# The PSUM banks that the transposes of v use in a gated DeltaNet and attention step

## The chip, the cores and the metric

One core of a Trainium2 chip runs the whole kernel. The metric is the device time of one execution in microseconds (us); the kernel before is given by the median of three executions.

## The reference

One inference step of a two-layer decoder trunk, for a prompt of 512 tokens and a sample group of 8 x 4 tokens that share the weights. Layer 0 is a gated DeltaNet, layer 1 a sliding-window attention, and each is followed by a SwiGLU block. The change lies in layer 0, which computes, cut to what matters:

```python
proj = h @ w_in                                   # 1024 -> q, k, v (8, 8, 16 heads of 128), z, b, a
qkv = silu(sum(full[:, k:k + L] * w[k] for k in range(4)))   # short causal convolution
q, k = l2norm(q) * 128 ** -0.5, l2norm(k)
Bm = strict(kb @ k.T * decay)                     # kb = k * beta, per chunk and head
T = inverse(I + Bm)                               # by doubling: M = -Bm, T = I + M, T += T @ M^(2^i)
u, w = T @ (v * beta), T @ (kb * exp(G))
for each chunk:                                   # the state S goes from chunk to chunk
    unew = u - w @ S
    o = (q * exp(G)) @ S + aqk @ unew
    S = S * exp(Gl) + (k * exp(Gl - G)).T @ unew
out = (rmsnorm(o) * silu(z)) @ w_out
```

## The kernel before, in words

Tokens lie along the free axis (544 columns: 512 of the prompt, 32 of the samples), cut into two halves of 256 and 288. Every large product is `dense` (L142): weights come in pieces of 128x512 over the SyncE queue, ScalarE rounds them to a high part and VectorE makes the low part (L133), and TensorE adds three products per weight block into one PSUM bank per half (L161). Tiles share the buffers in SBUF and the eight PSUM banks by tags. In the DeltaNet layer (L258) the banks are: `acc` three, for the halves of the projections; `t` two; `c` two; `v` one.

The DeltaNet work is cut into four groups g of two q/k heads and four v heads. Each group goes through steps, and the text `PLAN` (L39, L40) says in which order the steps are written down for all groups:

- kq (L587): the projections of k and q, each followed by `conv_silu` (L543): copies out of PSUM into a buffer `pre` (two of them), four taps into a buffer `y` (three of them; L559 on ScalarE, L561 on VectorE), a tanh (L563), and SiLU products (L571).
- t (L606): transposes of k and q, the Gram blocks with their decay (L692 to L705), the inverses of the 16x16 diagonal blocks on GpSimd, and for the samples a doubling product of 128x128 (L756 to L770). All of its PSUM tiles have the tag `t`; the last three are `pm`, `pm2` and `pm3`. `M1` (L765) is the sum that VectorE reads out of `pm2`, `TTs` (L770) the sum out of `pm3`. The small tiles MT, Mn and M1 have the SBUF tag `s128` with three buffers, which the sample step uses too (`rs`, L987).
- p and s (L920, L970): the products of the samples with their states, fed as small pieces between the blocks of other projections, and the rest of the samples' step.
- m (L774): the merge of the diagonal blocks into the inverse of 128x128. It is a chain of small products with a copy after each; its ten PSUM tiles all have the tag `v`, so each waits for the copy of the one before. Its last copy is L836.
- v (L838): for each of four heads a projection and `conv_silu`, whose result stays in `y`; four transposes of 128x128 into one bank `pv` (L849 to L851); and four copies by ScalarE, scaled by beta, into Vb (L854). Only then is `y` free. Vb is read by the chain of chunks.
- c (L857): the chain of the four chunks, with the tag `c`; z and o (L1024, L1041): the gate's projections and the output, of which z uses `pre` and no `y`.

The order on each engine is not that of the plan alone. The program writes the steps down in plan order, and a scheduler, which is told to use its own estimate of all durations (L1562), puts the instructions of each engine in an order in which steps overlap. Each engine then works strictly in that order, with waits on semaphores. A tile waits until a buffer of its tag is free. The lines around the change:

```python
PLAN = ("ba kq0 rn gt t0 p0 kq1 v0 s0 m0 t1 p1 c0 v1 kq2 z0 o0 s1 m1 t2 "
        "p2 c1 v2 kq3 z1 o1 s2 m2 t3 c2 v3 p3 z2 z3 o2 s3 m3 c3 wa wb o3")
```

Of the kernel before, what the change touches and what calls it, by code (L numbers as in the profile page):

```python
# [399 lines left out]
def gdn(ctx, tc, env):  # L400
    nc, PE, DVE, ACT, POOL = (env[k] for k in ("nc", "PE", "DVE", "ACT", "POOL"))
    tmp, bank, dense, halves = (env[k] for k in ("tmp", "bank", "dense", "halves"))
# [140 lines left out]
    def conv_silu(m, slot, cso, scst, emit, r=None):  # L543
        ps = dense(w_in[m], f"win{m}", hrhs, [8])
        pre = tmp("pre", f"pre{m}")
        pres = pre[:, YS:CONVW].rearrange("p (b t) -> p b t", t=3 + NT)
        POOL.memset(pre[:, 0:3], 0.0)
        POOL.tensor_copy(pres[:, :, 0:3], scst[:, slot].rearrange("p (b t) -> p b t", t=3))
        ACT.copy(pre[:, 3:3 + CUT], ps[0][:, :CUT])
        ACT.copy(pre[:, 3 + CUT:3 + SEQ], ps[1][:, :SEQ - CUT])  # L550
        ACT.copy(pres[:, :, 3:], ps[1][:, SEQ - CUT:TOK - CUT].rearrange("p (b t) -> p b t", t=NT))
        if r is not None:
            DVE.tensor_tensor(pre[:, 3:3 + SEQ], pre[:, 3:3 + SEQ], r[:, :SEQ], ALU.mult)
            DVE.tensor_tensor(pres[:, :, 3:], pres[:, :, 3:],
                              r[:, SEQ:].rearrange("p (b t) -> p b t", t=NT), ALU.mult)
        POOL.tensor_copy(cso[:, slot, 0:3], pre[:, SEQ:SEQ + 3])
        POOL.tensor_copy(cso[:, slot, 3:].rearrange("p (b t) -> p b t", t=3), pres[:, :, 4:7])
        y = tmp("y", f"y{m}")
        ACT.activation(y[:, :YW], pre[:, 0:YW], AF.Identity, scale=pc("taps", m * 4))  # L559
        for k in range(1, 4):  # L560
            DVE.scalar_tensor_tensor(y[:, :YW], pre[:, k:k + YW], pc("taps", m * 4 + k), y[:, :YW], ALU.mult, ALU.add)  # L561
        th = pre
        ACT.activation(th[:, :YW], y[:, :YW], AF.Tanh, scale=0.5)  # L563

        def srows(t):
            return t[:, YS:CONVW].rearrange("p (b t) -> p b t", t=3 + NT)[:, :, :NT]

        return emit(th, y, srows(th), srows(y))

    def sil(out, th, y):  # L570
        DVE.scalar_tensor_tensor(out, th, 1.0, y, ALU.add, ALU.mult)  # L571
# [266 lines left out]
    def proj_v(q):  # L838
        g = q.g
        q.Vb = [p2.tile([P, 4, P], F32, tag="Vb", name=f"Vb{g}_{n}", bufs=VBB) for n in range(NCH)]  # L840
        q.VS = p2.tile([P, 4, NB, NT], F32, tag="VS", name=f"VS{g}")
        for h in range(4):
            def emit(th, y, ths, ys):
                sil(q.VS[:, h], ths, ys)
                sil(y[:, :SEQ], th[:, :SEQ], y[:, :SEQ])
                return y

            VT = conv_silu(16 + 4 * g + h, 4 + h, q.cso, q.scst, emit)
            pv = bank("v", f"pv{g}_{h}")  # L849
            for n in range(NCH):  # L850
                PE.transpose(pv[:, n * P:(n + 1) * P], VT[:, n * P:(n + 1) * P], ident)  # L851
            for n in range(NCH):
                cc = n * 16 + 4 * g + h
                ACT.mul(q.Vb[n][:, h, :], pv[:, n * P:(n + 1) * P], col["bh"][:, cc:cc + 1])  # L854
        nc.gpsimd.dma_start(cs_out[:, 8 * g:8 * g + 8], q.cso)
# [272 lines left out]


    steps = {"kq": proj_kq, "t": tphase, "v": proj_v, "p": states, "s": sample, "m": merge, "c": chain, "z": proj_z, "o": out}  # L1130
    groups = {}
    for step in PLAN.split():
# [10 lines left out]
        else:  # L1143
            g = int(step[-1])
# [422 lines left out]
```

## Time and profile before

| what | value |
| --- | --- |
| median of three executions | 1694.58 us (1690.14 to 1696.34) |
| the profiled execution | 1703.09 us, of which its span is 1701.3 us |
| TensorE busy | 1634.9 us, 96% of the span |
| VectorE, ScalarE, GpSimd busy | 942.4, 753.6, 178.9 us |
| mean granted TensorE clock | 0.972 of full speed |

The span runs from the first to the last instruction of the profiled execution, and all places in the text are us from its start. In the tables PE is TensorE (PEld its weight loads, which overlap its products), DVE is VectorE, ACT is ScalarE, POOL is GpSimd. A row of a timeline has the start in us, the time that the merged instructions took, engine, line, operation, written tile and read tiles, shape and count; in brackets stands how long the engine was idle before and for whom it waited. The DeltaNet layer takes roughly the first 650 us.

### The profile page before, as it was taken

The numbers are of one execution on the slowest core, as the hardware profiler recorded it, in microseconds if no ns is written. First come the engines' busy times: TensorE is split into PE (matmuls) and PEld (weight loads), VectorE is DVE, ScalarE is ACT, GpSimd is POOL, SyncE is SP. The second block draws the span as 40 slices with busy tenths as digits, with TensorE's granted clock in tenths as the row PEclk, the third lists the DMA queues.
The fourth block names the chain that finished last, engine by engine and source line by source line (L and its number), as shares of the span: only waits on it lengthen the run. The fifth ranks groups of instructions, "written<-read, shape, count | busy, mean of one in ns | idle before, by whom it ended". The sixth has DMA issues, their size and how long they took to land.

```text
span 1701.3 us, 36800 instructions
## 1 busy us (share of the span) xinstructions
PE 1634.9 (96%) x14778; PEld 1574.8 (93%) x14778; DVE 942.4 (55%) x2089; ACT 753.6 (44%) x1826; POOL 178.9 (11%) x387
## 2 busy tenths in 40 slices
PE   7998988999999999999999999999999999999997
PEld 6898687898898898999999999999789999999997
DVE  6994574775656546554545433457666454544333
ACT  5765466665675354433333322246554333333221
POOL 3433132132121100100000000100000000000001
PEclk9999699999999999999999999999899999999998
DMA  6234333534436556523232333453112232223332
GB/s 230 77 109 120 107 73 124 155 62 161 145 81 186 175 148 194 183 87 93 88 88 88 87 87 91 125 146 117 28 50 82 88 87 87 88 90 90 87 90 82
DMA packets 156828, 186.06 MB, mean 109 GB/s; under 512 B 60928, under 2 KB 85552, under 8 KB 156656
## 3 DMA queue, kind: packets, MB, share of 16 engines
q1 hardware_dynamic: 148112, 161.98, 33.3%
q0 software_dynamic: 4416, 15.19, 2.5%
q10 hardware_dynamic: 4128, 6.53, 1.3%
q8 instruction: 116, 1.90, 0.5%
q14 instruction: 56, 0.46, 0.1%
HBM read 153.92 MB, written 24.49 MB: 105 GB/s over the span
## 4 chain that ended last, share of the span: by engine, by line
PE 82%; DMA 5%; DVE 4%; issue 3%; ACT 2%; POOL 2%; SPq 1%; POOLq 0%; ACTq 0%; DVEq 0%
PE wg_p L161 16%; PE wu_p L161 16%; PE wd_p L161 14%; PE win_p L161 6%; PE wo_p L161 6%; PE wz_p L161 4%; PE wqkv_p L161 4%; PE wao_p L161 3%; PE ptp L1296 1%; PE po L1302 1%; PE gram L692 1%; PE wdl_p L374 1%; DMA wk<-ksd 1%; PE pu L895 1%; PE po L866 1%
## 5 line engine op out<-in xcount | busy, mean ns | idle before, releaser
L161 PE MATMUL wu_p<-hl,wh_wu 128*128 128x256 f32 (+1 forms) x704 | 199.7, 288 | 0.0
L161 PE MATMUL wg_p<-hl,wh_wg 128*128 128x256 f32 (+1 forms) x704 | 199.7, 288 | 0.0
L161 PE MATMUL wg_p<-hh,wl_wg 128*128 128x256 f32 (+1 forms) x704 | 199.2, 287 | 0.0
L161 PE MATMUL wu_p<-hh,wl_wu 128*128 128x256 f32 (+1 forms) x704 | 199.1, 287 | 0.0
L161 PE MATMUL wg_p<-hh,wh_wg 128*128 128x256 f32 (+1 forms) x704 | 198.5, 288 | 0.3 <-DVE g L331 0.3
L161 PE MATMUL wu_p<-hh,wh_wu 128*128 128x256 f32 (+1 forms) x704 | 198.8, 288 | 0.0
L161 PE MATMUL wd_p<-al,wh_wd 128*128 128x256 f32 (+1 forms) x660 | 190.4, 289 | 0.0
L161 PE MATMUL wd_p<-ah,wl_wd 128*128 128x256 f32 (+1 forms) x660 | 190.1, 288 | 0.0
L161 PE MATMUL wd_p<-ah,wh_wd 128*128 128x256 f32 (+1 forms) x660 | 188.1, 285 | 0.0
L137 DVE TENSOR_TENSOR wl_wd<-wr_wd,wh_wd 128x512 fp32r<-128x512 f32 x90 | 58.3, 647 | 151.7 <-ACT wh_wd L135 150.6
L161 PE MATMUL win_p<-hl0n,wh_win 128*128 128x256 f32 (+1 forms) x448 | 136.9, 307 | 1.6 <-DVE hl0n L280 1.4
L161 PE MATMUL win_p<-hh0n,wl_win 128*128 128x256 f32 (+1 forms) x448 | 133.9, 302 | 2.5 <-DVE wl_win L137 2.5
L161 PE MATMUL win_p<-hh0n,wh_win 128*128 128x256 f32 (+1 forms) x448 | 135.2, 304 | 0.0
L135 ACT CAST wh_wg<-wr_wg 128x512 fp32r<-128x512 f32 x88 | 54.6, 620 | 178.9 <-PE wu_p L161 130.8
L161 PEld LDWEIGHTS wg_p<-hh,wh_wg 128*128 128x128 f32 x704 | 132.3, 188 | 0.4 <-DVE g L331 0.4
L161 PEld LDWEIGHTS wg_p<-hh,wl_wg 128*128 128x128 f32 x704 | 132.6, 189 | 0.0
L161 PEld LDWEIGHTS wu_p<-hh,wl_wu 128*128 128x128 f32 x704 | 132.6, 189 | 0.0
L161 PEld LDWEIGHTS wu_p<-hh,wh_wu 128*128 128x128 f32 x704 | 132.4, 188 | 0.0
L161 PEld LDWEIGHTS wg_p<-hl,wh_wg 128*128 128x128 f32 x704 | 132.4, 188 | 0.0
L161 PEld LDWEIGHTS wu_p<-hl,wh_wu 128*128 128x128 f32 x704 | 132.4, 188 | 0.0
L135 ACT CAST wh_wd<-wr_wd 128x512 fp32r<-128x512 f32 x90 | 52.7, 585 | 174.8 <-PE wd_p L161 153.7
L161 PEld LDWEIGHTS wd_p<-al,wh_wd 128*128 128x128 f32 x660 | 124.1, 188 | 0.0
(467 smaller groups left out, 4462.0 us busy)
## 6 DMA issues: line engine op xcount, KB each, us to landing
wr_wg<-in_w_gu SPq DMA_DIRECT2D x88, 256.0 KB
wr_wu<-in_w_gu SPq DMA_DIRECT2D x88, 256.0 KB
wr_wd<-in_w_dn SPq DMA_DIRECT2D x75, 256.0 KB
wr_win<-in_w_in SPq DMA_DIRECT2D x64, 256.0 KB
Sgp<-in_sdelta SPq DMA_DIRECT2D x16, 512.0 KB
Sgs<-in_sdelta SPq DMA_DIRECT2D x16, 512.0 KB
wr_wz<-in_w_in SPq DMA_DIRECT2D x32, 256.0 KB
out_ss<-Sgs POOLq DMA_DIRECT2D x16, 512.0 KB, 4.5
```

Of the source, the lines that this page charges most:

```text
L135: ACT.copy(hi[:, :n], raw[:, o:o + n])
L137: DVE.tensor_tensor(lo[:, :n], raw[:, o:o + n], hi[:, :n], ALU.subtract)
L161: PE.matmul(ps[f][:m, :hw(f)], lhsT=wt[:, sl], rhs=xt[:, hc(f)], start=(k0 + j == 0 and wi == 0), stop=(k0 + j == total - 1 and wi == 2),)
L374: PE.matmul(p, lhsT=wt[i][:, sl], rhs=xt[k][:, c], start=(k == 0 and wi == 0), stop=(k == KF - 1 and wi == 2))
L692: PE.matmul(gr[:, j * 256:(j + 1) * 256], lhsT=KQ[j][:, n, 0, :], rhs=KQ[j][:, n].rearrange("p a b -> p (a b)"), start=True, stop=True)
L866: PE.matmul(po[:, h * P:(h + 1) * P], lhsT=q.BA[n // 2][:, n % 2, h, 1, :], rhs=un[:, h], start=True, stop=True)
L895: PE.matmul(pu[:, h * P:(h + 1) * P], lhsT=q.BA[n // 2][:, n % 2, h, 0, :], rhs=V[:, h], start=True, stop=True)
L1296: PE.transpose(ptp[:, c * 256 + kb * P:c * 256 + (kb + 1) * P], s[:, c, n, kb * P:(kb + 1) * P], ident)
L1302: PE.matmul(po[rows, n * P:(n + 1) * P], lhsT=vt[:, n - 1 + kb, kv * 64:kv * 64 + 64], rhs=pT[:, c, kb * P:(kb + 1) * P], start=(kb == k0 ...
```

## The change

The four transposes of a v head go into a bank with the tag `t`, of which there are two, in place of the one with the tag `v`. Everything else stays: the pools, the plan, the merge, which is then alone on `v` after the start.

```diff
             VT = conv_silu(16 + 4 * g + h, 4 + h, q.cso, q.scst, emit)
-            pv = bank("v", f"pv{g}_{h}")
+            pv = bank("t", f"pv{g}_{h}")
             for n in range(NCH):
                 PE.transpose(pv[:, n * P:(n + 1) * P], VT[:, n * P:(n + 1) * P], ident)
```

## Rows read from the trace of the kernel before

**Rows 1.** The page: span, and busy time of the engines (share of the span, count).

```profile
span 1701.3 us, 36800 instructions
...
PE 1634.9 (96%) x14778; PEld 1574.8 (93%) x14778; DVE 942.4 (55%) x2089; ACT 753.6 (44%) x1826; POOL 178.9 (11%) x387
```

**Rows 2.** Busy time by stretches; first the length, PEclk is the mean granted clock.

```profile
core 0: us, PE busy (x) PEld busy (x) DVE busy (x) ACT busy (x) POOL busy (x), PEclk, DMA share, GB/s
98.00:123.00 25.00, 25.00 (x241) 23.26 (x240) 23.11 (x38) 16.19 (x42) 6.90 (x15) 1.00 0.45 131
157.00:171.00 14.00, 7.77 (x212) 6.70 (x210) 4.14 (x23) 5.29 (x10) 0.31 (x1) 0.86 0.60 133
171.00:212.00 41.00, 38.03 (x475) 28.09 (x475) 22.94 (x60) 18.63 (x49) 7.41 (x15) 0.63 0.36 110
212.00:235.00 23.00, 19.08 (x145) 18.21 (x145) 16.73 (x40) 17.06 (x60) 12.97 (x43) 1.00 0.23 29
300.00:361.00 61.00, 61.00 (x532) 55.82 (x531) 47.19 (x108) 41.86 (x120) 10.44 (x31) 1.00 0.43 126
361.00:368.00 7.00, 7.00 (x57) 6.89 (x56) 4.87 (x15) 5.77 (x19) 5.98 (x17) 1.00 0.12 38
```

**Rows 3.** Timeline of TensorE: the first transposes of v of groups 0 to 3.

```profile
98.30 0.60 PE L851 MATMUL pv<-kon,y 128*128 128x128 f32 x4
...
207.38 0.60 PE L851 MATMUL pv<-kon,y 128*128 128x128 f32 x4
...
333.45 0.49 PE L851 MATMUL pv<-kon,y 128*128 128x128 f32 x3
...
469.11 0.60 PE L851 MATMUL pv<-kon,y 128*128 128x128 f32 x4
```

**Rows 4.** Timeline of ScalarE: v0's last Vb copies, v1's first tanh, m0's last copy.

```profile
123.33 1.14 ACT L854 ACTIVATE Vb<-pv,c_bh 128x128 f32<-128x128 f32 x4 [1.12 <-PE pv L851]
...
125.48 0.68 ACT L563 ACTIVATE pre<-y 128x568 f32<-128x568 f32 x1
...
206.45 0.56 ACT L836 COPY BA<-py 64x512 f32<-64x512 f32 x1
```

**Rows 5.** Timelines of TensorE, VectorE and ScalarE: users of the tag s128.

```profile
131.83 0.38 PE L985 MATMUL pk<-kon,ksT 128*128 128x128 f32 x2
...
146.02 0.29 DVE L770 TENSOR_TENSOR TTs<-pm,MT 128x128 f32<-128x128 f32 x1 [2.47 <-PE pm L767]
...
146.19 0.36 ACT L987 ACTIVATE rs<-pk,c_bh 128x128 f32<-128x128 f32 x1
```

**Rows 6.** Timeline of ScalarE: copies of half projections, and the taps of v1's fourth head.

```profile
134.28 0.37 ACT L549 COPY pre<-win_p 128x256 f32<-128x256 f32 x1
...
209.03 0.79 ACT L559 ACTIVATE y<-pre,par 128x568 f32<-128x568 f32 x1
...
361.23 0.37 ACT L549 COPY pre<-win_p 128x256 f32<-128x256 f32 x1 [0.79 <-PE win_p L161]
```

**Rows 7.** Timeline of TensorE: the last projection product before the gap, the first after it.

```profile
163.56 0.36 PE L161 MATMUL win_p<-hh0n,wl_win 128*128 128x256 f32 x1
...
218.27 0.38 PE L161 MATMUL win_p<-hh0n,wh_win 128*128 128x288 f32 x1
```

**Rows 8.** Timeline of VectorE: the sum M1 of t0 to t3.

```profile
142.92 0.29 DVE L765 TENSOR_TENSOR M<-pm,MT 128x128 f32<-128x128 f32 x1
...
213.58 0.28 DVE L765 TENSOR_TENSOR M<-pm,MT 128x128 f32<-128x128 f32 x1
...
364.13 0.28 DVE L765 TENSOR_TENSOR M<-pm,MT 128x128 f32<-128x128 f32 x1
...
498.30 0.29 DVE L765 TENSOR_TENSOR M<-pm,MT 128x128 f32<-128x128 f32 x1
```

**Rows 9.** VectorE in a convolution: line L561 (ns min/median/max, starts), then two SiLU products.

```profile
L561 DVE SCALAR_TENSOR_TENSOR y<-pre,par,y x96: 791/802/812, 34.9 to 473.5; 128x568 f32<-128x568 f32 x96
...
126.19 0.19 DVE L571 SCALAR_TENSOR_TENSOR VS<-pre,y 128x32 f32<-128x32 f32 x1 [0.28 <-ACT pre L563]
126.31 0.68 DVE L571 SCALAR_TENSOR_TENSOR y<-pre,y 128x512 f32<-128x512 f32 x1
```

## The prediction

> **What bounds the kernel now.** I read the page first: TensorE is busy for 1634.9 of 1701.3 us [rows 1], so the end moves when TensorE's idle time, or its time at half clock, moves. The busy time by stretches shows where that is [rows 2]: 157 to 171 us has 14.00 - 7.77 = 6.2 us idle, 171 to 212 has 3.0 us idle and a mean granted clock of 0.63 (1.2 GHz for most of it, 2.4 GHz for the rest), 212 to 235 has 3.9 us idle. From 300 to 368 it is never idle.
>
> Why 157 to 235? Follow the transposes of v on TensorE [rows 3] and the rows ahead of them on ScalarE [rows 4]. Group 0's first transposes run at 98.30, as soon as their input is there. For group 1 the tanh of the first head ends at 125.48 + 0.68 = 126.2 and the only v bank is free at 123.33 + 1.14 = 124.5, yet the transposes wait until 207.38, behind the merge's last copy out of that bank (206.45 + 0.56 = 207.0). So a bank goes to the tiles of its tag in program order, whoever is ready first: m0 stands ahead of v1. The SBUF tag s128 says the same: `rs` of s0 has its input at 131.83 + 0.38 and runs at 146.19, right after t0's last tile user ends at 146.02 + 0.29 [rows 5]. While v1's transposes wait, three y buffers are held; the fourth head's taps run at 209.03 [rows 6], and no projection matmul runs between 163.56 and 218.27 [rows 7].
>
> **The change, part by part.** Nothing is added or removed: 64 transposes and 64 scaled copies as before. Their banks change, and with order of allocation the thing waited for: v(g) stands behind all of t(g) in the plan, so its first transposes need the bank that t(g)'s second doubling product frees, when its sum M1 has been read: 143.2, 213.9, 364.4 and 498.6 [rows 8], in place of 98.30, 207.38, 333.45 and 469.11 [rows 3]. All four are later: by 44.9, 6.5, 31.0 and 29.5 us. The merge gains nothing: when m(g) asks for its bank, v(g)'s last copies are long done, as for m0 (124.5).
>
> Price of a freed y: one convolution is taps 0.79 [rows 6], three multiply-adds of 0.80 [rows 9], tanh 0.68 [rows 4], two SiLU products of 0.68 and 0.19 [rows 9]: 4.7 us at least, before its `pre` buffer and then accumulator banks come free.
>
> *Group 0.* Three heads hold the y's; v0's fourth and v1's first sit in `pre`; v1's second fills two accumulators and half of v1's third the last, which came out at 134.28 [rows 6]. From there dense stands until 143.2 + 0.6 + 4.7 = 148.5: a hole of 14.2 us. I cost it at nothing, because the same four projections (they too end where the buffers are full) then run in 164 to 207, where dense has none now. Without that cover it is 14.2. Ends: 0 and +14; below zero is the second rival.
>
> *Group 1.* Release moves from 207.38 to 213.9, +6.5. Against it, t0 has VectorE more to itself (23.11 of 25.00 us busy at 98 to 123 [rows 2], with convolutions that now wait). For it, t1 must start after v0's last transposes: 148.5 + 0.6 in place of 146.3, +2.8. Ends: -6 (as far as t1 could run ahead) and +9. I take +3, nearer to the row of M1 than to the unseen speed-up.
>
> *Group 2.* Dense is at 100% here [rows 2], so a hole costs. The last half projection that fits came out at 361.23 [rows 6]; the y comes at 364.4 + 0.6, the `pre` at 369.7: a hole of 8.5 us. About half is filled by c1, which stands between t2 and v2 in the plan, is under way then, and would otherwise take TensorE later. I take +4; ends 0 (t2 ahead by as much) and +12 (no cover, and the clock falls: after the idle of 157 to 171 it stood at 0.63 over 41 us).
>
> *Group 3.* Behind v3 come z2 and z3, which need no y and can go on with the other `pre` buffer; Vb of group 3 is read by c3, after m3. Taken as 0, ends -1 and +3.
>
> *Two banks.* What could be gained directly is that a head's transposes no longer wait for the copies of the head before. In group 0 heads come one projection apart, so nothing waits. In group 1 three waits of at most 1.14 us [rows 4] could go. The Trainium skill (Perfetto Trace Analysis, section Matmuls) advises that independent groups rotate through PSUM banks so that one's evacuation overlaps the next one's matmuls. By that rule the sum would be 3.4 us less, +4 in place of +7; the trace agrees with the rule only where a bank is what is waited for, and that is an earlier tile of another step, not the neighbour. I take 0.
>
> Sum: 0 + 3 + 4 + 0 = **+7 us**. Made against the profiled execution, that is 1703.1 to 1710; against the median of the runs, 1694.6 (8.5 less), it is **1702**. With the ends of the terms its own range is about 1695 to 1709: some ends exclude each other, since a faster t0 helps both group 0 and group 1.
>
> **The rivals.** A measurement of this kernel can tell about 0.5%, 8.5 us: under 1686 is faster, over 1703 slower.
>
> *The hole of group 0 is not made up.* Place: 134 to 149. If the projections that move to 150 and later get between m0's steps and push m0 and t1 by as much, the 14.2 us stay: 1702 + 14 = 1716. For it: TensorE is full from 98 to 123 [rows 2] and works in its order, so each piece put in front of a merge step delays it. Against: 9.2 us idle and the half clock in 157 to 212 leave room. 0.20.
>
> *Faster: t0 and m0 move up.* Convolutions of three heads (v0's last, v1's first two) leave VectorE before 143, 3 x (2.4 + 0.68 + 0.19) = 9.8 us. If all of it shortens t0, then m0, which hangs on t0 through the DMAs of its blocks, and t1, which is woven into m0, end 9.8 us sooner: release at 213.9 - 9.8 = 204.1, 3.3 us ahead of now, and the projections fill the gaps at 157 to 171, so that the clock may hold. At 0.63 over 41 us up to 0.37 x 41 = 15 us are at stake; taking half, 3 + 7 = 10 us: 1685. It decides from the point where t1's M1 comes over 6.5 us earlier than 213.9. For it: VectorE at 92% in 98 to 123. Against: nothing shows that t0 waits for VectorE alone. 0.17.
>
> *The change does not do what I say: banks go to whoever is ready.* Then v1 is transposed at about 127, the y's come free and projections fill 164 to 218: idle 6.2 + 3.0 + 3.9 = 13 us and some half clock, so about 1680. Against it are the waits of rows 4 and 5. 0.03.
>
> *Nothing shows.* All the holes fall into waits that are there anyway, or t2 runs ahead as far as its cover went: 1694.6, give or take 3. For it: half of my sum is under the spread of the runs. 0.15.
>
> **How the numbers follow.** My forecast has 0.45: of its range 1695 to 1709 a little over half lies within 0.5% (0.26), the rest above (0.19). The first rival adds 0.20 to slower; the faster one 0.14 to faster and 0.03 to same; the third 0.03 to faster; the fourth 0.15 to same. Faster 0.17, same 0.44, slower 0.39. The range, 1688 to 1718, runs from the upper part of the faster rival to a little over the first; about 2 in 10 is left out.
>
> **What would show it.** In the changed profile, v's first transposes come just after the M1 sum of their own group's t step, at about 143, 210 to 214, 360 to 364 and 498; the taps of v0's fourth head move past 140; TensorE shows a hole near 134 to 149 and a smaller one near 361 to 370; 157 to 212 holds more projection matmuls. I am wrong if v1's transposes run before 200, if TensorE stays full at 134 to 149, or if m0's last copy (206.45) comes over 6.5 us sooner or later.

## The result and the profile after

The changed kernel takes 1724.23 us (median of four executions, 1719.41 to 1725.54), the kernel before 1695.46 us (four, 1690.14 to 1698.39): their medians lie 28.8 us, 1.7%, apart. The ratio on record for the pair is 1.0133, 95% interval 1.0094 to 1.0171, and the text goes by it: slower by about 1.3%, some 23 us by that ratio and 29 at the upper end of its interval, where I had forecast 7 us. The profiled execution took 1725.54 us, its span 1723.7.

The page after, answering to [rows 1]:

```profile
span 1723.7 us, 36805 instructions
...
PE 1635.9 (95%) x14778; PEld 1575.1 (91%) x14778; DVE 944.9 (55%) x2089; ACT 754.7 (44%) x1826; POOL 187.4 (11%) x387
```

TensorE works as long as before (1635.9 against 1634.9 us) in a span 22.4 us longer, so nearly all of the loss is idle time of TensorE. The busy time by stretches, columns as in [rows 2], shows where it lies. First after, then three stretches of the kernel before that [rows 2] doesn't have:

```profile
123.00:157.00 34.00, 22.62 (x153) 19.54 (x152) 18.62 (x39) 19.46 (x64) 14.57 (x40) 0.80 0.23 52
157.00:171.00 14.00, 10.10 (x189) 9.03 (x187) 4.90 (x11) 7.69 (x32) 1.48 (x6) 1.00 0.59 140
171.00:212.00 41.00, 36.36 (x575) 30.86 (x576) 21.15 (x69) 18.21 (x41) 7.70 (x17) 0.83 0.43 141
212.00:235.00 23.00, 19.23 (x132) 15.70 (x133) 16.07 (x40) 19.26 (x68) 7.36 (x20) 1.00 0.10 13
300.00:361.00 61.00, 61.00 (x602) 55.71 (x602) 41.25 (x108) 41.21 (x113) 9.91 (x24) 1.00 0.40 124
361.00:381.00 20.00, 13.89 (x120) 12.18 (x119) 13.65 (x33) 13.44 (x48) 11.05 (x33) 0.91 0.20 37
381.00:425.00 44.00, 38.62 (x381) 36.78 (x380) 28.50 (x56) 22.80 (x60) 10.25 (x15) 0.89 0.51 138
```

```profile
123.00:157.00 34.00, 34.00 (x283) 33.16 (x282) 21.26 (x45) 23.85 (x83) 13.06 (x45) 1.00 0.41 104
361.00:381.00 20.00, 19.99 (x158) 19.58 (x157) 13.22 (x33) 11.11 (x32) 11.39 (x35) 1.00 0.27 51
381.00:425.00 44.00, 41.33 (x718) 39.08 (x717) 24.88 (x52) 24.39 (x87) 9.79 (x18) 0.92 0.52 162
```

Two new holes: 34.00 - 22.62 = 11.4 us idle at 123 to 157, where TensorE had been full, and 6.1 us at 361 to 381, with 2.7 us more than before at 381 to 425. From 157 to 235 the idle time is 12.3 us, against 13.1 before: as idle time the first hole is hardly given back, though from 171 to 212 the mean granted clock is higher, 0.83 against 0.63.

The holes lie where the order of allocation puts them. TensorE's first transposes of v in groups 0 to 3, answering to [rows 3]:

```profile
137.43 1.92 PE L851 MATMUL pv<-kon,y 128*128 128x128 f32 x8
...
227.42 1.21 PE L851 MATMUL pv<-kon,y 128*128 128x128 f32 x8
...
369.52 0.60 PE L851 MATMUL pv<-kon,y 128*128 128x128 f32 x4
...
517.27 0.60 PE L851 MATMUL pv<-kon,y 128*128 128x128 f32 x4
```

and VectorE's sums M1 of t0 to t3, answering to [rows 8]:

```profile
136.50 0.29 DVE L765 TENSOR_TENSOR M<-pm,MT 128x128 f32<-128x128 f32 x1 [1.63 <-PE pm L763]
...
226.00 0.28 DVE L765 TENSOR_TENSOR M<-pm,MT 128x128 f32<-128x128 f32 x1
...
367.93 0.28 DVE L765 TENSOR_TENSOR M<-pm,MT 128x128 f32<-128x128 f32 x1
...
513.11 0.29 DVE L765 TENSOR_TENSOR M<-pm,MT 128x128 f32<-128x128 f32 x1 [0.95 <-PE pm L763]
```

In every group the transposes run 0.9 to 4.2 us after the M1 of their own group, and 20 to 48 us later than before. Group 0's first input (the SiLU product of its first head) ends at 95.50, as before (95.33), and its transposes come 39 us later. In the kernel before they did not quite run as soon as the input was there, but 3 us after it. What follows on ScalarE in group 0, answering to [rows 6] and to m0's last copy of [rows 4]:

```profile
112.33 0.37 ACT L549 COPY pre<-win_p 128x256 f32<-128x256 f32 x1 [0.66 <-ACT E L704]
...
139.54 0.78 ACT L559 ACTIVATE y<-pre,par 128x568 f32<-128x568 f32 x1
140.20 1.16 ACT L854 ACTIVATE Vb<-pv,c_bh 128x128 f32<-128x128 f32 x4
141.21 0.81 ACT L559 ACTIVATE y<-pre,par 128x568 f32<-128x568 f32 x1
...
146.13 0.37 ACT L549 COPY pre<-win_p 128x256 f32<-128x256 f32 x1
...
213.10 0.58 ACT L836 COPY BA<-py 64x512 f32<-64x512 f32 x1 [1.54 <-PE py L835]
```

No half projection is copied out between 112.7 and 146.13. The last projection products before each hole and the first behind it, on TensorE:

```profile
128.94 0.28 PE L161 MATMUL win_p<-hh0n,wl_win 128*128 128x256 f32 x1
...
147.78 0.59 PE L161 MATMUL win_p<-hh0n,wh_win 128*128 128x288 f32 x1
...
363.25 0.28 PE L161 MATMUL win_p<-hh0n,wl_win 128*128 128x256 f32 x1
...
381.64 0.61 PE L161 MATMUL win_p<-hh0n,wh_win 128*128 128x288 f32 x1
```

The projections stand still for 18.6 us in group 0 and 18.1 us in group 2, where I had worked out 14.2 and 8.5.

### The profile page after: what moved, and what is told of

Read it like the earlier page. It is cut to its first block, busy times and chain, and to the rows that moved or that the text cites. A ratio compares the mean times of both kernels' runs of the same rounds, so it can differ in the third digit from the quotient of the medians.

```text
span 1723.7 us, 36805 instructions
## 1 busy us (share of the span) xinstructions
PE 1635.9 (95%) x14778; PEld 1575.1 (91%) x14778; DVE 944.9 (55%) x2089; ACT 754.7 (44%) x1826; POOL 187.4 (11%) x387
## 4 chain that ended last, share of the span: by engine, by line
PE 80%; DMA 6%; DVE 5%; POOL 3%; ACT 2%; issue 2%; SPq 1%; POOLq 0%; ACTq 0%; DVEq 0%
PE wg_p L161 15%; PE wu_p L161 15%; PE wd_p L161 14%; PE win_p L161 8%; PE wo_p L161 6%; PE wqkv_p L161 4%; PE wz_p L161 4%; PE wao_p L161 3%; POOL LT L741 1%; POOL subt L739 1%; PE po L1302 1%; DMA Sgp<-in_sdelta 1%; PE wdl_p L374 1%; PE ptp L1296 1%; PE gram L692 1%
```

## The experiments

Runs of the kernel before scatter by some 25 us among themselves (1684 to 1709 us over one series of 35). So verdicts rest on the timed ratios with their 95% intervals, and the traces, one execution each, tell places and orders; the traced execution of the kernel before is one of its longer ones (1703.09 us).

**One group at a time.** The change for one group alone; `g == 0` becomes 1, 2 and 3 in the others.

```diff
-            pv = bank("v", f"pv{g}_{h}")
+            pv = bank("t" if g == 0 else "v", f"pv{g}_{h}")
```

> Only group 0's transposes of v use the banks of the t step, groups 1 to 3 keep the merge's bank. Theory 1 (transposes now stand behind the whole t step of their group; the projections stop where the three y buffers are held, and that costs only where nothing else makes it up): the hole at about 129 to 146 us is there as in the changed kernel, but it is made up before 235, so the time is within 0.4% of before (0 to +6 us). Theory 2 (the tiles of v in the t banks delay the next t step, whose row transposes for the decay came 17 us later in group 1 of the changed kernel): this group alone carries the larger part, +10 us or more. Theory 3 (any other order of the schedule costs something, whichever group): about a quarter of the 29 us, +7.

> Only group 1's transposes of v use the banks of the t step. Theory 1: they wait for the sum M1 of t1 (213.9 us before) in place of the merge's last copy (207.0), 6 us later, and the merge and the chain beside them leave room: 0 to +5 us. Theory 2: no delay of a t step here, since t2 comes 60 us later: 0. Theory 3: +7.

> Only group 2's transposes of v use the banks of the t step. Theory 1: this is where TensorE had no idle time before (300 to 381 us); the projections stop for some 18 us after about 347 to 361, and the time is 14 to 24 us over before, most of what the whole change costs. Theory 2: 0 to +4. Theory 3: +7.

> Only group 3's transposes of v use the banks of the t step. Theory 1: behind them come the projections of the gate, which need no y; 0 to +4 us. Theory 2: 0, there is no next t step. Theory 3: +7.

Measured: group 0 1.0055 [1.003, 1.008], group 1 0.9999 [0.9969, 1.0029], group 2 1.004 [1.0007, 1.0072], group 3 0.9983 [0.9955, 1.0011]. Group 0, which I had costed at nothing, costs about 9 us by itself (5 to 14 by the interval), between what theories 1 and 2 allowed it; its transposes run at 136.2, and TensorE's idle time from 98 to 160 grows from 2.6 to 11.7 us. Group 1 costs nothing that shows. Group 2 costs about 7 us, half or less of the 14 to 24 that I expected here.

**Pairs, and all but one.** The same edit with `g in (0, 1)`, `g in (2, 3)`, `g != 0` and `g != 3`.

> Groups 0 and 1 transpose v in the banks of the t step, 2 and 3 in the merge's. Theory A (the costs of the groups add up): 0.55% + 0 = 1.0055 of before, 1705 us. Theory B (group 0 alone pushes t1: its M1 came at 233.8 us in place of 213.6, which cost little while v1 stood behind the merge, at 211.8; with both groups changed v1 stands behind that late M1): v1's first transposes at 225 to 234, 14 to 22 us later than with group 0 alone, and most of it in the time: 1.010 to 1.014, 1712 to 1719 us, so that these two groups carry most of the whole change.

> Groups 2 and 3 transpose v in the banks of the t step. Theory A: 0.40% - 0.17% = 1.002, 1699 us. Theory B: group 2's late v2 pushes kq3 and with it t3, behind whose M1 v3 then stands; but the gate's projections lie behind v3, so no more than +3 us over the sum: 1.002 to 1.004. A rival that puts the loss of the whole change into group 2 would need 1.009 or more here.

> The changed kernel with the v transposes of group 0 alone left on the merge's bank; groups 1, 2 and 3 use the t banks. It tells whether group 0's share is its own or comes through a larger hole in group 2. Theory A (shares add): the whole's +1.33% less group 0's +0.58% (the mean of its two runs, 0.55 and 0.62) leaves +0.75%, a ratio of about 1.0075, and m0 takes 32 to 38 us as before, with its last copy near 206. Theory B (groups 0 and 1 make t2 late, and only this makes group 2's hole large): with group 0 back, t2 is on time, and what is left is what group 2 cost alone, 1.004 or less; M1 of t2 near 351 and projections back by 372 to 375 us instead of 381.

> The changed kernel with the v transposes of group 3 alone left on the merge's bank. It tells whether group 3, which I had costed at nothing, has a share of the +1.33%. Theory A: group 3 costs nothing (alone it measured 0.9983), so the ratio stays at about 1.013. Theory B: group 3 is the difference between groups 2 and 3 together (1.0067) and group 2 alone (1.004), so the ratio falls to about 1.0105.

Measured: groups 0 and 1 1.0062 [1.0034, 1.0089], groups 2 and 3 1.0067 [1.004, 1.0095], all but group 0 1.0095 [1.0061, 1.0128], all but group 3 1.0083 [1.0052, 1.0114]. With groups 0 and 1 changed, v1's transposes do come later than with group 0 alone (225.09 against 211.76), yet no time goes with it. The halves add up, within wide intervals: 0.62% + 0.67% = 1.29%, the whole being 1.33%. Groups 2 and 3 together came out over both of my theories (1.002, and 1.002 to 1.004); all but group 3 lies under theory A's 1.013 and fits theory B's 1.0105.

The idea that group 2's hole is large only because the groups ahead make t2 late has fallen in the form it was put. It wanted 1.004 or less for all but group 0, and 1.0095 was measured; the trace shows the hole there too, though M1 of t2 comes at 358.01, ten microseconds sooner than in the changed kernel. On ScalarE, the taps of the next two heads and the next copy of a half projection:

```profile
361.74 0.81 ACT L559 ACTIVATE y<-pre,par 128x568 f32<-128x568 f32 x1
...
363.88 0.85 ACT L559 ACTIVATE y<-pre,par 128x568 f32<-128x568 f32 x1
...
370.40 0.35 ACT L549 COPY pre<-win_p 128x256 f32<-128x256 f32 x1
```

From M1 to that copy it takes 12.4 us (358.01 to 370.40). In the changed kernel it takes 13.3 us (367.93 to 381.24), with group 2 alone 12.3 us (349.04 to 361.29), with groups 2 and 3 12.2, with all but group 3 13.0. So the end of the hole hangs on M1 by a nearly fixed distance; I had put it at 0.6 + 4.7 = 5.3 us.

If the shares of the four groups simply add, the nine ratios (these eight and the whole) give, by least squares weighted with their intervals, 0.48, 0.09, 0.51 and 0.12%, each within 0.2: 8, 1.5, 9 and 2 us. The largest misfit is two standard errors, in group 3 alone. Whether group 3 has a share stays open: alone it measured -0.17%, and its removal from the whole took off 0.5%, with an interval of 0.5 either way.

**m0's length.** These traces also bear on the first rival: projections that group 0 pushes behind 150 get between m0's steps. From VectorE's read of m0's first product (L786) to the start of ScalarE's last copy (L836), with the projection products that TensorE ran in that time:

| kernels | projection products inside m0 | m0, us |
| --- | --- | --- |
| before; group 1, 2, 3 alone; groups 2 and 3; all but group 0 | 0 in each | 37.6; 38.1, 32.2, 35.8; 33.0; 37.7 |
| group 0 alone; groups 0 and 1; all but group 3; the changed kernel | 89 in each | 42.5; 42.2; 42.0; 42.2 |
| the kernel before with `vt`, the changed kernel with `vt` (next part) | 0, 62 | 42.7, 37.4 |
| two accumulators: merge's bank, own bank (further down) | 113, 171 | 44.8, 53.3 |

In the first ten kernels, which differ in the groups alone, 89 products inside m0 go with an m0 that is some 4 to 10 us longer. The pair with `vt` breaks the pattern: none inside and as long, 62 inside and no longer. So products inside m0 go with a longer m0 in most of these kernels, but that they alone set its length isn't shown.

Nor is it shown that a long m0 is what costs the time. Group 0 also makes t1 late (M1 of t1 at 222 to 234 us in the four kernels of the second row, 207 to 214 in the six of the first), which was theory 2 of its run. In the two kernels of the last row m0 is longer still and M1 of t1 comes at 230, and they lose 0.2 and 0.4%. And the kernel before with `vt` has a hole too, 34.00 - 24.39 = 9.6 us idle in 123 to 157, and loses nothing (0.9999). So of the late t1, the long m0 and the hole, none costs 0.5% by itself in every kernel that has it. That group 0's banks cost some 9 us is measured; by which of these paths stays open.

**What the held tiles do.** In the first try the SiLU of v goes to a tile of its own with one buffer, so that the y is free while the transposes wait (VS, BAs and TTs go down to one buffer to pay for it). It was done to both kernels.

```diff
-                sil(y[:, :SEQ], th[:, :SEQ], y[:, :SEQ])
-                return y
+                vt = p2.tile([P, SEQ], F32, tag="vt", name=f"vt{g}_{h}", bufs=1)
+                sil(vt, th[:, :SEQ], y[:, :SEQ])
+                return vt
```

> The changed kernel, with the SiLU product of v going into a buffer of its own (one, tag vt) in place of y, paid for by one buffer in place of two for VS, BAs and TTs. If the cost is that waiting transposes hold the y buffers, each head but one still holds a y, and one more convolution and projection (6.4 us at full clock) runs before the projections stop: holes of groups 0 and 2 some 6 us shorter, the time 6 to 13 us under the changed kernel, 1711 to 1718 us. If what costs is only the place of the tiles in the t tag (late t1 and nothing else), the time stays at 1724 +- 4.

> The kernel before with the same extra buffer and the same three single buffers: the control of the run above. v1's transposes wait for the merge with three y held here too, so by the same theory projections run some 6 us further into the gap at 164 to 218 us: 0 to -6 us. If the single buffers cost something, it shows as a slower time.

Measured: the changed kernel with it 1.0235 [1.0199, 1.027], the kernel before with it 0.9999 [0.9975, 1.0023]. The first is a miss: it got slower by 1%. With one `vt` buffer the product itself has to wait for the transposes of the head before, and while it waits it keeps `pre` as well as y. The second half of v0's fourth projection is copied out at 132.40, where the changed kernel has it at 107.79. (v0's second head shows it: its small product runs at 102.15, the one into `vt` at 131.14, after the first head's transposes at 130.04.) So it moved the shortage, and did not take it away. That the same edit is free in the kernel before, where three groups of four don't wait, fits the wait for the transposes as the cause, but doesn't show it.

The second try has a fourth y buffer, in both kernels (VS, BAs, TTs and the attention's bias tile have one buffer for it).

```diff
-        return tpool.tile([P, CONVW + 5], F32, tag=tag, name=name, bufs=3 if tag == "y" else PREB)
+        return tpool.tile([P, CONVW + 5], F32, tag=tag, name=name, bufs=4 if tag == "y" else PREB)
```

> The changed kernel with four y buffers in place of three, paid for by one buffer in place of two for VS, BAs, TTs and the attention's bias. If the cost comes from the y and pre buffers that waiting heads hold, the fourth head of v goes on and with it one more projection or two (6 to 13 us): v0's fourth head gets its taps at about 107 in place of 139, kq3's second head is copied before 370 in place of 381, and the time falls from 1724 to 1708 to 1716. If the cost is only that v and t steps take turns at the banks of t, buffers change nothing: 1720 to 1728.

> The control: the kernel before with four y buffers and the same four single buffers. v1's transposes still wait for the merge, with one more projection in the gap at 164 to 218 us. By the buffer theory 0 to -6 us against before; the price of the single buffers, if any, shows as a slower time.

Measured: 1.0073 [1.0053, 1.0094] for the changed kernel, 0.6% or 10 us less than without it (1.0133), and 0.9945 [0.9919, 0.997] for the kernel before. The first, 1710 us, lies in the range that the buffer theory gave, the second somewhat past its 0 to -6 us. The projections move up as they should: v1's second is copied out from 122.37 in place of 146.13. But both kernels gain, so the ratio between the two, 1.0073 / 0.9945 = 1.0129, is that of the change as it was. The y tiles are short in both, and a fourth doesn't undo what the change costs. With it the kernel before is the fastest measured here, 1688.07 us.

**Which wait it is.** In three kernels one accumulator bank is given up. In the first the free bank is v's own; in the second it stands idle and v uses the `t` banks; in the third it stands idle and v uses the merge's bank, as before.

```diff
-        psum_pools(gctx, acc=3, t=2, c=2, v=1)
+        psum_pools(gctx, acc=2, t=2, c=2, v=1, w=1)
...
-            pv = bank("v", f"pv{g}_{h}")
+            pv = bank("w", f"pv{g}_{h}")
```

> The projections have two banks in place of three, and the transposes of v one bank of their own. By the order of allocation they wait for nobody: v0's first at about 97, v1's first at about 127 (the next heads of v1 then wait for a Vb buffer, which the chain c0 frees at about 200), v2's at about 310, v3's at about 440. Two banks cost the projections something, I guess 1 to 3%. Against the run beside it, which differs in the tag alone: 0.5 to 1.5% faster. If order of allocation is not the cause, the transposes come where they came before and the two runs agree.

> The same banks (two for the projections, one that stays empty), with the transposes of v in the two banks of the t step, as in the change. They run only after M1 of their own t step, as in the changed kernel, and the time is 0.5 to 1.5% over the run beside it.

> The control of the two kernels with two accumulator banks: the kernel before with one accumulator bank less (the bank stands idle) and the v transposes on the merge's bank as they were. Theory A (a bank of their own lets the transposes run at once, frees the y tiles early and gains time, but the lost accumulator eats it): the accumulator's price is that of the pair with the t banks, 1.023 against 1.0133, about 1%, so 1.010 here, and the own bank's gain is 1.010 less 1.0042 = 0.6%. Theory B (the early transposes are worth nothing, since the heads then wait for the Vb buffers anyway): 1.004, the same as with the own bank.

Measured: own bank 1.0042 [1.0021, 1.0062], `t` banks 1.023 [1.0206, 1.0253], merge's bank 1.0019 [0.9995, 1.0044]. The first transposes of the four groups in the kernel with an own bank:

```profile
114.25 0.60 PE L851 MATMUL pv<-kon,y 128*128 128x128 f32 x4
...
143.23 0.39 PE L851 MATMUL pv<-kon,y 128*128 128x128 f32 x2
...
303.28 0.60 PE L851 MATMUL pv<-kon,y 128*128 128x128 f32 x4
...
441.19 0.65 PE L851 MATMUL pv<-kon,y 128*128 128x128 f32 x4
```

They wait neither for t nor for m. In the kernel with the idle bank and the `t` banks the same rows begin at 137.90, 225.88, 372.45 and 522.02. The two differ in that bank alone, and by 33.6 us (1736.97 against 1703.37). That is 1.9%, more than the 0.5 to 1.5% that I expected, and with the merge's bank the gap is as large. So what the change costs time by is that v's transposes share the tag `t`. The sharing works both ways, v behind t of its own group and the next t behind v; these runs don't part the two, though a late t1 alone (230 us with the own bank and with the merge's) costs little.

An accumulator fewer costs 0.2% with v on the merge's bank (1.0019) and about 1% with v on the `t` banks (1.023 against 1.0133). But here is a second miss of mine: with two accumulators a bank of its own gains nothing over the merge's bank (1.0042 against 1.0019). Freeing v1's first head from m0, at 143 in place of 208.51, is worth nothing that can be measured. The trace says why. Of the first head's four copies into Vb three run at 145.51 to 146.70, and the fourth only here:

```profile
202.59 0.37 ACT L854 ACTIVATE Vb<-pv,c_bh 128x128 f32<-128x128 f32 x1
```

There are seven Vb buffers and a group takes four. The fourth of v1 comes free when c0's first chunk has read its Vb (L895, 201.49 to 202.55). Until then the bank is held, and v1's second head is transposed at 204.85, hardly sooner than v1's first with the merge's bank (208.51). So the bank of its own let one head of v1 through, as I had written ahead of the run; one with more Vb buffers wasn't made.

> A try for a better version: the v transposes in a bank of their own (one accumulator bank less) and a fourth y buffer (paid with single buffers of VS, BAs, TTs and the attention's bias). Theory A (the y tiles are still short, as a projection waits for one somewhere else than at v): the fourth y gains its 0.55% again, 1.0042 - 0.0055 = 0.9987. Theory B (with transposes that wait for nobody no y is held for long, and the accumulators are what is short): the fourth y is worth nothing, 1.004. Either way the fourth y alone with three accumulators, 0.9945, should stay the best.

Own bank and fourth y together (the two diffs above) measured 1.0029 [1.0005, 1.0052]: the fourth y gains little on top of the own bank. Nothing beats the kernel before with a fourth y.

## Why the prediction was wrong in size

**What held.** Banks of a tag go in program order. The four waits are where I put them, behind M1 of the own group, though M1 itself came at 226 and 513 in groups 1 and 3 where I had 214 and 498. The taps of v0's fourth head (139.54) were expected past 140. There is a hole near 134 to 149, out of which the projections came at 147.78 (I had 148.5), and one near 361 to 370, and 157 to 212 holds more projections. The direction held. That two banks give nothing by themselves was not tested. One of my signs of being wrong came, just so: m0's last copy is 6.65 us later (213.10 in place of 206.45), and I had named 6.5.

The time, 1724, is past my range, which ended at 1718. The ends of my four terms add up to -7 and +38, or 1688 to 1733; I had narrowed that to 1695 to 1709 with the reason that some ends exclude each other, which speaks of the low ends alone.

**The step that failed: group 0.** I had written of the 14.2 us "I cost it at nothing, because the same four projections (...) then run in 164 to 207, where dense has none now". They do run there: the 89 products. But they make up the hole in part only: group 0 alone costs 0.55%, about 9 us of the 14.2 that the first rival, which I gave 0.20, asked for. The idle time in 157 to 235 fell by 0.8 us only (13.1 to 12.3).

Most of the cover came from the clock. In 171 to 212 the mean granted clock rose from 0.63 to 0.83, nearer to 2.4 GHz, while in 123 to 157, where TensorE now idles, it fell from 1.00 to 0.80, which I had not costed. A rough estimate takes the busy time of each stretch times its mean clock: 123 to 157 loses 34.0 - 18.1 = 15.9 us of work at full clock, and 157 to 235 wins back 59.5 - 49.7 = 9.8. Some 6 us stay. Over the whole span the clock is the same, 0.973 against 0.972.

So I was wrong to count all idle and half-clock time there as room. Why the idle part was not filled is not settled. The first rival's mechanism, products that hold up m0's steps, fits m0's 42 us in the four kernels with group 0 on the `t` banks and three y, but the table on m0 has kernels that don't follow it.

**Mis-sized: group 2**, +4, measured at 7 us alone and about 9 by the fit. The hole is 18.1 us and not 8.5. It ends 381.64 - 369.7 = 11.9 us later than I had it, by three parts. M1 is 3.8 us later (367.93 in place of 364.13), since t2 itself is late. From M1 to the taps it takes 3.8 us (367.93 to 371.72) where I had the 0.6 us of the transposes; ScalarE has other work in between. And the convolution takes some 9 us where I had the sum of its durations, 4.7:

```profile
368.98 0.31 ACT L1049 ACTIVATE jo<-KQ 128x128 bf16<-128x128 f32 x1
...
369.72 1.12 ACT L892 ACTIVATE KQ<-pq,c_eG 128x128 f32<-128x128 f32 x4
370.72 1.16 ACT L854 ACTIVATE Vb<-pv,c_bh 128x128 f32<-128x128 f32 x4
371.72 0.81 ACT L559 ACTIVATE y<-pre,par 128x568 f32<-128x568 f32 x1
372.38 0.63 ACT L897 COPY un<-pu 128x512 f32<-128x512 f32 x1
372.84 1.21 ACT L854 ACTIVATE Vb<-pv,c_bh 128x128 f32<-128x128 f32 x4
373.86 0.85 ACT L559 ACTIVATE y<-pre,par 128x568 f32<-128x568 f32 x1
...
376.19 0.68 ACT L563 ACTIVATE pre<-y 128x568 f32<-128x568 f32 x1 [0.45 <-DVE y L561]
```

```profile
372.57 1.66 DVE L561 SCALAR_TENSOR_TENSOR y<-pre,par,y 128x568 f32<-128x568 f32 x2 [2.55 <-ACT y L559]
374.26 1.12 DVE L904 SCALAR_TENSOR_TENSOR S<-S,c_eGl,pS 128x128 f32<-128x128 f32 x4
375.30 1.52 DVE L561 SCALAR_TENSOR_TENSOR y<-pre,par,y 128x568 f32<-128x568 f32 x2
378.19 0.38 DVE L743 COPY LT<-LT 128x256 f32<-128x256 f32 x1 [1.37 <-POOL LT L741]
378.48 0.68 DVE L869 TENSOR_TENSOR KQ<-po,KQ 128x512 f32<-128x512 f32 x1
379.08 0.80 DVE L561 SCALAR_TENSOR_TENSOR y<-pre,par,y 128x568 f32<-128x568 f32 x1
379.80 0.18 DVE L571 SCALAR_TENSOR_TENSOR VS<-pre,y 128x32 f32<-128x32 f32 x1
379.90 0.68 DVE L571 SCALAR_TENSOR_TENSOR y<-pre,y 128x512 f32<-128x512 f32 x1
```

Three heads get their transposes within 3 us, so two convolutions start at once and their multiply-adds share VectorE with c1, which I had named as the cover of the hole. It did cover the hole, and more than the half that I gave it (TensorE was idle for 6.1 us in 361 to 381), but its steps on VectorE stand between those of the convolutions. So does a copy of the t step (L743), for which VectorE sits idle 1.37 us until GpSimd is done: the first head's tanh ends at 376.87, and its SiLU product starts at 379.80. The lateness of t2 is no large part of the cost: with group 0 put back, M1 of t2 came at 358.01, sooner than the 364.13 of before, and groups 1 to 3 together still lost 0.95%.

**Group 1**, +3 with ends -6 and +9: nothing to 1.5 us. M1 of t1 came at 226.00, 12 us past my release, so the place was wrong by more than the time; that didn't show in the time, and the projections catch up in the stretch behind (v2's last head is copied out at 332.0 with groups 0 and 1 changed, at 333.7 with group 0 alone). **Group 3**, 0 with an end of +3: 2 us by the fit, not settled.

**The faster rival** was right in its first step alone. t0's M1 came at 136.50 in place of 142.92, 6.4 us sooner, with VectorE less busy ahead of it (20.61 of 25.00 us in 98 to 123, in place of 23.11); that the one comes of the other isn't shown. m0 did not follow: its first product was read at 170.90, against 168.83, and it then took 42.2 us in place of 37.6.

## What to carry to other kernels

Before you give a tile a tag with more buffers, list what stands ahead of it in that tag in program order: two banks shared with a step that ends late can cost more than a single one shared with a step that is done. Idle and half-clock time further on isn't a full cover for a new hole: here, by a rough estimate, 10 us of 16 came back. Before you give a tile a bank of its own, look which buffer it waits for next. And when a wait releases several tiles at once, cost what follows as a queue on the engines it shares, and not as the sum of one piece's durations.

## What the runs showed of the hardware that was not expected

TensorE's transposes took over half as long again inside the new hole: eight of them 1.92 us at 137.43, against 1.21 us for eight at 227.42. The granted clock was 0.50 (1.2 GHz) from 137.40 to 139.40 and 1.00 (2.4 GHz) from 227.40 to 228.70; the first stretch lies in a hole in which TensorE had already been idle for part of the time.

One accumulator bank out of three could be given up for 0.2%, within the interval of no change, as long as v kept the merge's bank.
